# A diffusion layer in three-pass matmuls: the first up blocks reordered, the last output tile split over two free banks

## The chip, the cores and the metric

The kernel runs on one core of one Trainium2 chip. The metric is the device time of one execution in microseconds (us); for the kernel before it is the median of three runs. PE is TensorE's matmul row and PEld its weight loads, DVE is VectorE, ACT is ScalarE, POOL is GpSimd, and SP is SyncE, which here issues nearly all DMAs. SBUF is the on-chip working memory, PSUM the eight accumulation banks that PE writes.

## The reference, cut to what matters

One layer of a diffusion backbone over 1024 latent tokens of width 1024 with 256 context tokens, in float32. Two token mixers (retention and differential attention) are followed by an output projection, a norm, a gated feed-forward block with a convolution over the tokens, and a final norm. The change touches only what comes from the second norm on:

```python
def conv_ffn(h, w_up, conv_w, conv_b, w_down):
    u = h @ w_up                                   # (1024, 1024) @ (1024, 5632)
    up = jnp.pad(u, ((0, 0), (1, 1), (0, 0)))
    u = up[:, :-2] * conv_w[0] + up[:, 1:-1] * conv_w[1] + up[:, 2:] * conv_w[2] + conv_b
    a, b = jnp.split(u, 2, axis=-1)
    return (jax.nn.silu(a) * b) @ w_down           # (1024, 2816) @ (2816, 1024)

    h2 = rms_norm(x, norm2_g[l]) * (1.0 + sc2) + sh2
    x = x + g2 * conv_ffn(h2, w_up[l], conv_w[l], conv_b[l], w_down[l])
    return rms_norm(x, final_g)
```

## The kernel before, in words

**Arithmetic.** A float32 operand is split into a high part (a cast to fp32r on ACT, L1008) and a low part (the difference, on DVE, L1009); `passes` (L129 to L131) multiplies high by high, high by low and low by high into one PSUM bank. So a product of 128 x 512 over an inner size of 512 is 12 matmuls. Both projections of the feed-forward block use a seven-product (Strassen-like) scheme on halves, so the operands of products are sums and differences of quadrants of activations and weights.

**Up blocks.** There are 22 blocks of 128 output columns (`Block`, j = 0 to 21). For block j two weight tiles are loaded, `wra` (the columns of the gate half) and `wrb` (those of the other half), each 128 x 8 x 128. For j = 0 and 1 POOL forms the sums of weights ahead (`sums_in_place`); from j = NSUM = 2 on `combined` (L1163 to L1166) forms four of them on POOL, s1 = b1 + b2 first. The right weights of block 2 have a place of their own, `third_b`, which lies in memory that the first activation quadrants occupied. `begin` computes p1 and p2; `first_sum` copies the bank `chain` to `ua` (L1149) and adds p2 on DVE (L1150). `middle` adds p6 to the same bank, copies it to the right half of `ua` (L1250), adds p7 and copies it to the right half of `ub` (L1258). `end` adds p3 and p4 and finishes `ua` (L1265) and the left half of `ub` (L1266). A bank that is copied can be added to only when the copy is done. `ua` has two buffers, so block j + 2 takes that of block j. `gated` runs the convolution of both halves (ACT L1201, DVE L1202 and L1203), Silu on ACT (L1271), the product (L1272) and the stores of sums for the down projection (`down_operands`). In the loop the order is begin(j), end(j - 1), gated(j - 1), middle(j). The first three blocks' p1 and p2 and the third and fifth products of blocks 0 and 1 are computed earlier, while the turned activations T1 to T4 are still being split (`turned1`).

**Down projection.** Four phases over M = 11 pairs of blocks follow, each on the eight banks `c1` and `c2` (four row tiles each). Phase one multiplies a11 and a12 with the left weights, phases two and three the stored sums with differences of weights (`first_difference`, `less`), phase four the pair a22. All four quadrants of w_down for a pair, `W[m, r, c]`, are loaded in phase one's loop (L1351) and stay. At phase ends banks are copied or added into `acc`, one tile per 128 rows. `residual` loads the old row half from x1_d (L1380), multiplies by the gate and adds (L1382, L1383), and squares on ACT (L1385); `rstd` adds the two halves' sums (L1388) and takes the power on POOL (L115); `scaled` multiplies by the root and by the final gain and stores (L1393, L1394). In phase four the last four pairs are done tile by tile, so that four tiles of the lower half end one after another; tile 7 is the last.

**Order.** Instructions of one engine run in order. The order on each engine comes from a planner, which weighs costs and due times, except where `in_order` ties each instruction to the one before it on its engine (PE, DVE, ACT, SP). SP's queue is in order too: a DMA that waits for a buffer holds those behind it.

Of the kernel before, what the change touches and what calls it, by code (L numbers as in the profile page):

```python
# [8 lines left out]
F32 = mybir.dt.float32  # L9
# [3 lines left out]
ALU = mybir.AluOpType  # L13
# [59 lines left out]
def kernel(  # L73
# [39 lines left out]
    def rsqrt(out_ap, in_ap, mul, eps, n):  # L113
        nc.vector.tensor_scalar(out=out_ap, in0=in_ap, scalar1=mul, scalar2=eps, op0=ALU.mult, op1=ALU.add)  # L114
        nc.gpsimd.tensor_tensor(out=out_ap, in0=out_ap, in1=mhalf[:, :n], op=ALU.pow)  # L115

    def in_order(start):
        last = {}
        for ins in nc.cur_bb.bb.instructions[start:]:
            if ins.engine not in FORCE:  # L120
                continue
            if ins.engine in last:
                tc.add_manual_dep(ins, last[ins.engine].name, mybir.DependencyInfo(mybir.DependencyClass.NoSync, mybir.DependencyReason.DATA), reason="order")
            last[ins.engine] = ins
# [879 lines left out]

    def split_op(src):
        hi = wop.tile([P, 4, P], F32R, name="whi")
        lo = wop.tile([P, 4, P], F32R, name="wlo")
        nc.scalar.copy(hi, src)  # L1008
        nc.vector.tensor_tensor(out=lo, in0=src, in1=r32(hi), op=ALU.subtract)  # L1009
        return hi, lo  # L1010

    def raw_load(name, src, pool=None):
        o = (pool or wst).tile([P, KD, P], F32, name=name)
        nc.sync.dma_start(out=o, in_=src)
        return o
# [15 lines left out]
    xo = x1lS.enter_context(tc.tile_pool(name="xo", bufs=1, side="right"))  # L1031
    x1 = [(x1lp if t < 4 else x1hp).tile([P, D], F32, name=f"x1_{t}") for t in range(NT)]
    raw0 = rwp.tile([P, KD, 512], F32, name="raw0")
# [4 lines left out]
    def norm2(t):  # L1038
        nc.sync.dma_start(out=x1_d[t], in_=x1[t])
        sq = xo.tile([P, D], BF16, name="sq2")  # L1040
        nc.scalar.activation(sq, x1[t], AF.Square, accum_out=sm2[:, t : t + 1])
# [153 lines left out]
    with ExitStack() as p4:  # L1195
# [9 lines left out]

        third_b = p4.enter_context(tc.tile_pool(name="third_b", bufs=1, side="right", reuse_waits="tile"))
        raws.append(up_load(NSUM))
        held = {}

# [18 lines left out]
        class Block:  # L1228
# [4 lines left out]
            def op(self, p):  # L1233
                return split_op(self.ops[p])

# [11 lines left out]
            def middle(self):  # L1247
                j = self.j
                product(self.chain, self.op("p6"), T2, False)
                nc.scalar.copy(self.ua[:, 512:], self.chain)  # L1250
# [7 lines left out]
                nc.scalar.copy(self.ub[:, 512:], self.chain)  # L1258
                nc.vector.tensor_tensor(out=self.ub[:, 512:], in0=self.fifth, in1=self.ub[:, 512:], op=ALU.add)
# [7 lines left out]

            def gated(self):
                ta = conv(self.ua, self.j)
                tb = conv(self.ub, self.j + NF)  # L1270
                nc.scalar.activation(ta, ta, AF.Silu)  # L1271
                nc.vector.tensor_tensor(out=ta, in0=ta, in1=tb, op=ALU.mult)  # L1272
                down_operands(self.j, ta)

        last = None
        for j in range(NF):
            if NSUM < j + 1 < NF:
                raws.append(up_load(j + 1))
            blk = Block(j)
            blk.begin()  # L1280
            if last is not None:
                last.end()
                last.gated()
            blk.middle()
            last = blk
        last.end()
# [17 lines left out]
        for m in range(2):  # L1304
# [5 lines left out]
            for i, cc in enumerate((c1, c2)):  # L1310
                step(cc, split1(pa[:, i * C : (i + 1) * C]), split1(pb[:, i * C : (i + 1) * C]), m == 0, False)
        last.gated()
    ctx_t.close()
    ctx_y.close()
    ctx_ya.close()

    with ExitStack() as p5:
# [28 lines left out]
        W = {}  # L1346
        for m in range(2, M + 2):
            m %= M
            for r, c in ((0, 0), (1, 0), (0, 1), (1, 1)):
                W[m, r, c] = resident(F32)  # L1350
                nc.sync.dma_start(out=W[m, r, c], in_=w_down[2 * m + r][:, c * C : (c + 1) * C])  # L1351
            if m >= 2:
                a11, a12 = a_pair(0, m, alone=m < 4)
                step(c1, a11, split1(W[m, 0, 0]), False, m == M - 1)
                step(c2, a12, split1(W[m, 1, 0]), False, m == M - 1)
            if m >= 6:
                first_difference(m - 4)
        first_difference(0)
        first_difference(1)

# [4 lines left out]
        nc.sync.dma_start(out=fg, in_=rows[0, R_FG : R_FG + D].partition_broadcast(P))  # L1365
        sm4 = fin.tile([P, NT, 2], F32, name="sm4")
        halves = [slice(0, C), slice(C, D)]
# [9 lines left out]

        def residual(t, c, src=None):
            xt = fin.tile([P, C], F32, name="x1t", bufs=4)
            nc.sync.dma_start(out=xt, in_=x1_d[t][:, halves[c]])  # L1380
            dst = acc[t][:, halves[c]]
            nc.vector.tensor_tensor(out=dst, in0=dst if src is None else src, in1=g2bc[:, halves[c]], op=ALU.mult)  # L1382
            nc.vector.tensor_tensor(out=dst, in0=dst, in1=xt, op=ALU.add)  # L1383
            jk = fin.tile([P, C], BF16, name="jk", bufs=2)
            nc.scalar.activation(jk, dst, AF.Square, accum_out=sm4[:, t, c : c + 1])  # L1385

        def rstd(t):
            nc.vector.tensor_tensor(out=sm4[:, t, 0:1], in0=sm4[:, t, 0:1], in1=sm4[:, t, 1:2], op=ALU.add)  # L1388
            rsqrt(sm4[:, t, 0:1], sm4[:, t, 0:1], 1.0 / D, EPS, 1)

        def scaled(t, c0, c1_):
            x_ = acc[t][:, c0:c1_]
            nc.vector.scalar_tensor_tensor(out=x_, in0=x_, scalar=sm4[:, t, 0:1], in1=fg[:, c0:c1_], op0=ALU.mult, op1=ALU.mult)  # L1393
            nc.sync.dma_start(out=out[t * P : (t + 1) * P, c0:c1_], in_=x_)  # L1394
# [5 lines left out]
        for m in range(M):  # L1400
# [14 lines left out]
        for m in range(M):  # L1415
# [7 lines left out]
            T4s.append((hi, lo))  # L1423
        add_to(c1, 1, 1)
        add_to(c2, 0, 1)

        def rows_before(m):
            if m < 4:
                residual(m, 1)
                rstd(m)  # L1430
                scaled(m, 0, D)
                residual(4 + m, 1)
                dst = acc[4 + m][:, C:]
                nc.vector.tensor_tensor(out=dst, in0=dst, in1=fg[:, C:], op=ALU.mult)

        a22s = []
# [5 lines left out]
        late_ops = list(zip(a22s, T4s))[M - 4 :]  # L1442
        for t in range(4):
            for i, ops in enumerate(late_ops):
                step(c1, *ops, False, i == 3, True, [t])
            r = 4 + t
            residual(r, 0, c1[t])
            rstd(r)
            nc.scalar.activation(acc[r][:, C:], acc[r][:, C:], AF.Copy, scale=sm4[:, r, 0:1])
            nc.sync.dma_start(out=out[r * P : (r + 1) * P, C:], in_=acc[r][:, C:])  # L1450
            scaled(r, 0, C)

# [81 lines left out]
```

## Time and profile before

| what | us |
|---|---|
| median of 3 runs (1408.39 to 1412.42) | 1408.58 |
| the profiled execution, its own time | 1407.91 |
| its span | 1406.1 |
| busy DVE, ACT, POOL in the span | 991.4, 729.6, 287.5 |
| mean granted clock of TensorE | 0.995 |

A profile is of one execution. A line of the timeline gives start, duration, engine, source line, operation, output <- inputs, shape, and in brackets how long the engine was idle before it and what released it. A group line gives a count, busy us and mean ns of one, then the idle time before. Lines of DMA issues give the size and the median us from issue to landing. PE's matmul of 512 columns shows a duration of about 0.39 us, but the matmuls overlap: a new one starts every 0.23 us, and that step is what counts.

### The profile page before, as it was taken

The page shows a single profiled execution, that of the slowest core. Times are in us where ns is not written, and L with a number is a line of the kernel's source. Part 1 is how long each engine was busy: PE and PEld are TensorE (multiplying, and loading weights), DVE is VectorE, ACT ScalarE, POOL GpSimd, SP SyncE. Part 2 cuts the span into 40 slices and gives each one's busy share as a digit, 9 for nine tenths or more (in the row PEclk, how much of TensorE's full clock was granted, in tenths as well). Part 3 has the DMA queues.
Part 4 walks back from the last instruction along what each step waited for, and adds up shares of the span by engine and source line. Part 5 has one row for each costly group of instructions (what it writes and reads, how often), then busy time and mean ns, then how long its engine had stood idle before and what let it go on. Part 6 is the DMA issues. An engine that isn't in the chain of part 4 may idle for free.

```text
span 1406.1 us, 19426 instructions
## 1 busy us (share of the span) xinstructions
PE 1366.5 (97%) x7028; PEld 1147.6 (82%) x7028; DVE 991.4 (71%) x1445; ACT 729.6 (52%) x1391; POOL 287.5 (20%) x321
## 2 busy tenths in 40 slices
PE   8899999999999899999999999999999999999996
PEld 5688888888887799998888778888888888888885
DVE  3655874424686798886458987777787777897457
ACT  3553313333575689997136645555445555455533
POOL 1310000001656033411201242233332220000001
PEclk9999999999999999999999999999999999999999
DMA  9546885465575597622321223323323226953224
GB/s 336 224 151 200 284 278 188 134 182 172 177 242 159 175 208 170 126 66 85 141 98 45 97 98 113 113 90 113 105 105 113 96 79 219 397 175 104 91 97 179
DMA packets 96807, 218.81 MB, mean 156 GB/s; under 512 B 9220, under 2 KB 31236, under 8 KB 96200
## 3 DMA queue, kind: packets, MB, share of 16 engines
q1 hardware_dynamic: 88552, 192.67, 40.0%
q0 software_dynamic: 8160, 24.91, 7.8%
q8 instruction: 55, 0.90, 0.3%
q14 instruction: 40, 0.33, 0.1%
HBM read 160.13 MB, written 57.41 MB: 155 GB/s over the span
## 4 chain that ended last, share of the span: by engine, by line
PE 81%; issue 5%; DMA 5%; DVE 4%; ACT 2%; POOL 2%; SPq 0%; POOLq 0%; ACTq 0%; DVEq 0%
PE pv L869 5%; PE chain L129 5%; PE pA L837 5%; PE chain L131 5%; PE chain L130 5%; PE c L131 4%; PE c L129 4%; PE c L130 4%; PE pn L129 4%; PE pn L131 4%; PE pn L130 3%; PE pl L129 3%; PE pl L131 3%; PE pl L130 3%; PE third L129 2%
## 5 line engine op out<-in xcount | busy, mean ns | idle before, releaser
L129 PE MATMUL chain<-T,whi 128*128 128x512 f32 x264 | 103.5, 393 | 4.9 <-ACT ua L1250 3.9
L129 PE MATMUL pl<-hT,whi 128*128 128x512 f32 x256 | 106.2, 415 | 0.0
L130 PE MATMUL chain<-T,whi 128*128 128x512 f32 x264 | 103.5, 392 | 0.0
L131 PE MATMUL chain<-T,wlo 128*128 128x512 f32 x264 | 103.3, 392 | 0.0
L131 PE MATMUL pl<-hT,wlo 128*128 128x512 f32 x256 | 100.2, 391 | 0.0
L130 PE MATMUL pl<-hT,whi 128*128 128x512 f32 x256 | 100.0, 391 | 0.0
L840 DVE TENSOR_REDUCE mt<-pA 128x1 f32<-128x1280 f32 x64 | 95.3, 1490 | 3.6 <-PE pA L837 2.8
L837 PE MATMUL pA<-ks,qhl 128*128 128x512 f32 (+1 forms) x384 | 89.5, 369 | 2.7 <-ACT p L844 2.7
L131 PE MATMUL c<-whi,ghl 128*128 128x512 f32 x232 | 90.4, 390 | 0.0
L130 PE MATMUL c<-wlo,ghl 128*128 128x512 f32 x232 | 90.3, 389 | 0.0
L129 PE MATMUL c<-whi,ghl 128*128 128x512 f32 x232 | 90.3, 389 | 0.0
L844 ACT ACTIVATE p<-pA,mt 128x1280 f32<-128x1280 f32 x64 | 85.5, 1336 | 6.7 <-DVE mt L840 6.7
L1008 ACT CAST whi<-cmb 128x512 fp32r<-128x512 f32 x62 | 38.6, 623 | 86.7 <-PE chain L130 65.3
L837 PEld LDWEIGHTS pA<-ks,qhl 128*128 128x128 f32 x384 | 67.6, 189 | 14.8 <-ACT p L844 3.4
L129 PE MATMUL pn<-whi,hT 128*128 128x512 f32 x192 | 79.1, 412 | 0.0
L1163 POOL TENSOR_TENSOR cmb<-wrb 128x512 f32<-128x512 f32 x20 | 27.2, 1360 | 248.7 <-DMA wrb<-w_up 165.6
L869 PE MATMUL pv<-va,aT 128*128 128x128 f32 x640 | 77.0, 275 | 0.1
L131 PE MATMUL pn<-whi,hT 128*128 128x512 f32 x192 | 75.6, 394 | 0.9 <-POOL hT L552 0.4
L130 PE MATMUL pn<-wlo,hT 128*128 128x512 f32 x192 | 75.6, 394 | 0.0
L869 PEld LDWEIGHTS pv<-va,aT 128*128 128x128 f32 x640 | 74.0, 192 | 0.7 <-DVE yT L898 0.3
L1009 DVE TENSOR_TENSOR wlo<-cmb,whi 128x512 fp32r<-128x512 f32 x62 | 57.0, 922 | 23.0 <-ACT whi L1008 23.0
L115 POOL TENSOR_TENSOR sm<-sm,mhalf 128x1 f32<-128x1 f32 x26 | 17.0, 657 | 274.0 <-DVE sm L114 273.9
(300 smaller groups left out, 3812.7 us busy)
## 6 DMA issues: line engine op xcount, KB each, us to landing
wm<-w_mod SPq DMA_DIRECT2D x32, 512.0 KB, 5.1
raw<-w_in SPq DMA_DIRECT2D x27, 512.0 KB, 4.6
wra<-w_up SPq DMA_DIRECT2D x24, 512.0 KB, 3.4
wrb<-w_up SPq DMA_DIRECT2D x23, 512.0 KB, 3.5
W<-w_down SPq DMA_DIRECT2D x44, 256.0 KB, 6.2
ad<-s SPq DMA_DIRECT2D x20, 512.0 KB, 3.6
wra<-ad SPq DMA_DIRECT2D x20, 512.0 KB, 3.3
kvs<-kvg SPq DMA_DIRECT2D x36, 256.0 KB, 3.2
```

The lines of the kernel that those rows point to most:

```text
L115: nc.gpsimd.tensor_tensor(out=out_ap, in0=out_ap, in1=mhalf[:, :n], op=ALU.pow)
L129: mm(ps, lh, rh, start=first, stop=False, skip_group_check=more)
L130: mm(ps, lh, rl, start=False, stop=False, skip_group_check=more)
L131: mm(ps, ll, rh, start=False, stop=last, skip_group_check=more)
L837: mm(self.pa[m][:, c0:c1], self.q[:, m, i, qs], self.k[:, m, c0:c1], start=(i == 0), stop=(i == 1))
L840: nc.vector.tensor_reduce(out=self.mt[:, m : m + 1], in_=self.pa[m][:, :LK], axis=AX.X, op=ALU.min)
L844: nc.scalar.activation(self.p[m], self.pa[m][:, :LK], AF.Exp, scale=-1.0, bias=self.mt[:, m : m + 1], accum_out=self.s[:, m : m + 1])
L869: mm(self.pv, self.aT[:, c, :], self.v[:, c, :], start=(c == 0), stop=(c == NKT - 1))
L1008: nc.scalar.copy(hi, src)
L1009: nc.vector.tensor_tensor(out=lo, in0=src, in1=r32(hi), op=ALU.subtract)
L1163: nc.gpsimd.tensor_tensor(out=s1, in0=b1, in1=b2, op=ALU.add)
```

## The change

- `up_load(NSUM)`: block 2's right weights go into x1[7], the last row tile of the normed activations, which gets a pool of its own (`x1k`) and is kept to the end of the up blocks; `third_b` goes. The load is issued right after the first third products instead of after the pools of the first stage are closed. Its order against the left weights is no longer tied.
- The casts of block 2 are ordered behind block 0's copy of p7's bank (`copied[0]`).
- For j = 1, 2, 3 the call `last.gated()` moves behind `blk.middle()`, and its Silu is ordered behind the copy after p6 of block j (`blk.copied`).
- A one-column Silu is run on ACT in the first `norm2`, so that the table is loaded there.
- w_down: phase one loads only the left quadrants, the right ones (c = 1) for three pairs at its end and then for pair m + 3 in phase two, with `first_difference(m + 1)` there.
- `residual` is taken apart: `old_row` (load), `gated_row` (multiply and add), `squares`. Right halves of all eight tiles get gate and old row in phase three, left halves of tiles 0 to 3 too; what phase three adds is multiplied by the gate straight from the bank (`gated_more`) and added later (`add_more`). `rstd` takes the sum and the division in one instruction, with eps added ahead (`with_eps`).
- The end: tiles 4 to 6 as before, the four old rows loaded ahead; tile 7's part so far is taken from `c1[3]`, and its last four products go as two quarters of 256 columns into `c2[0]` and `c2[1]`. Its right half is stored from ACT's queue. The whole end is tied by `in_order`.

```diff
+    keptp = ctx.enter_context(ExitStack())
+    x1k = keptp.enter_context(tc.tile_pool(name="x1k", bufs=1, side="right", reuse_waits="tile"))
...
+    x1.append(x1k.tile([P, D], F32, name="x1_7"))
...
+        if t == 0:
+            nc.scalar.activation(sm2[:, 32:33], sm2[:, 0:1], AF.Silu)
...
         if j == NSUM:
-            start = len(nc.cur_bb.bb.instructions)
-            b = raw_load("wrb", w_up[j + NF], third_b)
-            a = raw_load("wra", w_up[j])
-            in_order(start)
-            return a, b
+            b = raw_load("wrb", w_up[j + NF], x1[NT - 1].rearrange("p (k l) -> p k l", k=KD))
+            return raw_load("wra", w_up[j]), b
...
     beside(iter(()), 0.0)
+    raws.append(up_load(NSUM))
     tmpS.close()
     rawp.close()
...
             def op(self, p):
-                return split_op(self.ops[p])
+                return split_op(self.ops[p], copied[0] if self.j == NSUM else None)
...
-            def gated(self):
+            def gated(self, after=None):
                 ta = conv(self.ua, self.j)
                 tb = conv(self.ub, self.j + NF)
-                nc.scalar.activation(ta, ta, AF.Silu)
+                silu = nc.scalar.activation(ta, ta, AF.Silu)
+                if after is not None:
+                    order_only(silu.ins, after.ins)
...
+            late_gate = 0 < j < 4
...
             if last is not None:
                 last.end()
-                last.gated()
+                if not late_gate:
+                    last.gated()
             blk.middle()
+            if late_gate:
+                last.gated(blk.copied)
...
+        for m in range(2, M):
+            load_W(m, 0)
+            a11, a12 = a_pair(0, m, alone=m < 4)
+            step(c1, a11, split1(W[m, 0, 0]), False, m == M - 1)
+            step(c2, a12, split1(W[m, 1, 0]), False, m == M - 1)
+        for m in range(2):
+            load_W(m, 0)
+        for m in range(3):
+            load_W(m, 1)
         first_difference(0)
...
-            if m < 4:
-                first_difference(M - 4 + m)
-            if 2 <= m < 6:
-                residual(m - 2, 0)
+            if m + 3 < M:
+                load_W(m + 3, 1)
+            if m + 1 < M:
+                first_difference(m + 1)
...
-        add_to(c1, 1, 1)
-        add_to(c2, 0, 1)
+            if m < NT:
+                t = (m + 4) % NT
+                gated_row(t, halves[1], acc[t][:, C:], old_row(t, 1))
+            if 2 <= m < 6:
+                gated_row(m - 2, halves[0], acc[m - 2][:, :C], old_row(m - 2, 0))
+                squares(m - 2, halves[0], 0)
+        late_rows = gated_more(c1, 1)
+        for row in late_rows:
+            add_more(*row)
+        first_rows = gated_more(c2, 0)
...
+        for n in range(2):
+            part = slice(n * C // 2, (n + 1) * C // 2)
+            for i, (a, b) in enumerate(late_ops):
+                passes(c2[n][:, : C // 2], tuple(g[:, 3 * P :] for g in a), tuple(g[:, part] for g in b), i == 0, i == 3)
+            gated_row(NT - 1, part, c2[n][:, : C // 2], acc[NT - 1][:, part], more[:, part])
+            squares(NT - 1, part, 2 * n)
+            if n == 0:
+                finish(NT - 2)
+                add_squares(NT - 1)
+        rstd(NT - 1, 2)
+        finish(NT - 1)
+        in_order(begin)
```

The helpers that are new: `order_only(a, b)` puts a behind b in the order without a semaphore; `finish(r)` scales and stores both halves of tile r; `gated_row`, `squares`, `gated_more`, `add_more` and `with_eps` are told above.

More of the change, by code (lines that the diff above doesn't have):

```diff
@@ L115, in rsqrt, with order_only @@
         nc.gpsimd.tensor_tensor(out=out_ap, in0=out_ap, in1=mhalf[:, :n], op=ALU.pow)
+    def order_only(ins, before):
+        tc.add_manual_dep(ins, before.name, mybir.DependencyInfo(mybir.DependencyClass.NoSync, mybir.DependencyReason.DATA), reason="order")
     def in_order(start):
@@ L122, in in_order @@
             if ins.engine in last:
-                tc.add_manual_dep(ins, last[ins.engine].name, mybir.DependencyInfo(mybir.DependencyClass.NoSync, mybir.DependencyReason.DATA), reason="order")
+                order_only(ins, last[ins.engine])
             last[ins.engine] = ins
@@ L1031 @@
     xo = x1lS.enter_context(tc.tile_pool(name="xo", bufs=1, side="right"))
-    x1 = [(x1lp if t < 4 else x1hp).tile([P, D], F32, name=f"x1_{t}") for t in range(NT)]
+    x1 = [(x1lp if t < 4 else x1hp).tile([P, D], F32, name=f"x1_{t}") for t in range(NT - 1)]
+    x1.append(x1k.tile([P, D], F32, name="x1_7"))
     raw0 = rwp.tile([P, KD, 512], F32, name="raw0")
@@ L1204, in conv @@
             return t
-        third_b = p4.enter_context(tc.tile_pool(name="third_b", bufs=1, side="right", reuse_waits="tile"))
-        raws.append(up_load(NSUM))
-        held = {}
+        held, copied = {}, []
         def down_operands(j, g):
@@ L1249, in middle @@
                 product(self.chain, self.op("p6"), T2, False)
-                nc.scalar.copy(self.ua[:, 512:], self.chain)
+                self.copied = nc.scalar.copy(self.ua[:, 512:], self.chain)
                 if j < NSUM:
@@ L1312 @@
         last.gated()
+    keptp.close()
     ctx_t.close()
@@ L1384, in residual, with squares @@
+        def squares(t, cols, i):
+            n = cols.stop - cols.start
             jk = fin.tile([P, C], BF16, name="jk", bufs=2)
[L1385 to L1389, printed above, removed]
+            nc.scalar.activation(jk[:, :n], acc[t][:, cols], AF.Square, accum_out=sm4[:, t, i : i + 1])
@@ new lines, in gated_row, with gated_more @@
+        def gated_row(t, cols, src, xt, tmp=None):
+            dst = acc[t][:, cols]
+            tmp = dst if tmp is None else tmp
+            nc.vector.tensor_tensor(out=tmp, in0=src, in1=g2bc[:, cols], op=ALU.mult)
+            nc.vector.tensor_tensor(out=dst, in0=tmp, in1=xt, op=ALU.add)
+        def gated_more(pd, r):
+            tmps = [fin.tile([P, C], F32, name="more", bufs=4) for _ in range(4)]
+            for t in range(4):
+                nc.vector.tensor_tensor(out=tmps[t], in0=pd[t], in1=g2bc[:, C:], op=ALU.mult)
+            return [(4 * r + t, tmps[t]) for t in range(4)]
@@ L1442, with finish @@
         late_ops = list(zip(a22s, T4s))[M - 4 :]
[L1443 removed]
+        olds = [old_row(4 + t, 0) for t in range(4)]
+        more = fin.tile([P, C], F32, name="more", bufs=4)
+        def finish(r):
+            nc.scalar.activation(acc[r][:, C:], acc[r][:, C:], AF.Copy, scale=sm4[:, r, 3:4])
+            (nc.scalar if r == NT - 1 else nc.sync).dma_start(out=out[r * P : (r + 1) * P, C:], in_=acc[r][:, C:])
+            scaled(r, 0, C)
+        begin = len(nc.cur_bb.bb.instructions)
+        for t in range(3):
+            r = 4 + t
             for i, ops in enumerate(late_ops):
                 step(c1, *ops, False, i == 3, True, [t])
[L1446 to L1451 removed]
+            gated_row(r, halves[0], c1[t], olds[t])
+            squares(r, halves[0], 0)
+            if t:
+                finish(r - 1)
+            else:
+                with_eps(NT - 1)
+                gated_row(NT - 1, halves[0], c1[3], olds[3])
+            rstd(r)
+        for n in range(2):
[10 more added lines that the diff above has]
+        in_order(begin)
 def shape_constants():
```

54 lines of the change are left out of this document (31 added, 23 removed).

## The prediction

> **What bounds the kernel now.** I read the page first: engine shares, then the forty slices.
>
> ```profile
> PE 1366.5 (97%) x7028; PEld 1147.6 (82%) x7028; DVE 991.4 (71%) x1445; ACT 729.6 (52%) x1391; POOL 287.5 (20%) x321
> ```
>
> PE is busy 97% of the 1406.1 us span, so a change that removes no matmul can only win what PE loses in waits. The change touches nothing before about 700 us; I therefore cut the rest of the span into stretches of 10 us. These are the only stretches behind 760 us in which PE loses more than 0.2 us (columns: stretch and its length, then busy us of PE, PEld, DVE, ACT, POOL, the granted clock, the DMA share, GB/s):
>
> ```profile
> 790.00:800.00 10.00, 7.13 (x31) 5.28 (x30) 7.41 (x7) 6.63 (x9) 8.81 (x6) 1.00 0.59 222
> 830.00:840.00 10.00, 8.08 (x28) 6.48 (x29) 7.18 (x10) 4.50 (x8) 3.01 (x2) 0.83 0.24 82
> 1390.00:1400.00 10.00, 4.86 (x22) 3.69 (x20) 8.34 (x18) 4.70 (x11) 2.10 (x3) 0.98 0.48 180
> 1400.00:1406.10 6.10, 0.00 (x0) 0.00 (x0) 1.06 (x3) 0.89 (x3) 0.55 (x1) 0.50 0.46 172
> ```
>
> Two losses sit at the start of the up blocks (one of them with a lowered clock), one at the end. The view of waits, for PE from 740 us on, has two lines in all:
>
> ```profile
> PE chain L129 <- ACT ua L1250: 3.9, 2, 2.1
> PE chain L129 <- ACT ub L1258: 1.0, 1, 1.0
> ```
>
> All three waits are for ScalarE's copy of a bank which PE wants to go on adding to. Between 840 and 1390 us, where phases one to four of the down projection lie, there is nothing to win, only to lose.
>
> **First stalls (790 to 800 us).** Timeline of ACT, and of PE at the second stall:
>
> ```profile
> 792.88 0.62 ACT L1008 CAST whi<-cmb 128x512 fp32r<-128x512 f32 x1 [1.06 <-POOL cmb L1164]
> 793.40 0.58 ACT L1258 COPY ub<-chain 128x512 f32<-128x512 f32 x1
> 796.22 1.28 ACT L1271 ACT_TABLE_LOAD   x1 [1.72 <-DVE tconv L1203]
> 798.95 0.59 ACT L1250 COPY ua<-chain 128x512 f32<-128x512 f32 x1
> 797.34 0.39 PE L131 MATMUL chain<-T,wlo 128*128 128x512 f32 x1
> 799.59 0.50 PE L129 MATMUL chain<-T,whi 128*128 128x512 f32 x1 [1.86 <-ACT ua L1250]
> ```
>
> ACT works in order. Block 0's copy (793.40) stands behind a cast for block 2 that waits for a sum on POOL; block 1's copy (798.95) stands behind a table load and a Silu that wait for DVE's convolution. The change puts the casts of block 2 behind the first copy, the Silu behind the second, and pulls the table load forward to the first norm. The built order agrees: ACT now has copy, cast, cast, block 2's first copy, cast, copy, copy, then convolution and Silu.
>
> The 1.0 us wait goes. The 2.0 us wait (799.59 less 797.34 less one matmul of 0.23) does not go wholly, because ACT now stands one step earlier: block 2's first copy writes the buffer of block 0, which is free only when DVE has read it.
>
> ```profile
> 794.62 1.52 DVE L1203 SCALAR_TENSOR_TENSOR tconv<-ua,cl,tconv 128x1023 f32<-128x1023 f32 x1
> ```
>
> That is at 796.14. The copy (0.58) ends near 796.7, and a cast, a copy and block 1's copy follow at about 0.5 each, the last done near 798.3. PE has its next matmuls (four of block 1, four of block 2, then block 1's next product) waiting from 796.2: gaps of about 0.5 and 0.6, and perhaps 0.1 behind the Silu, 1.2 in place of 3.0. That is 1.8 us won.
>
> **What the early load of block 2 costs.** Its right weights now go into x1[7], free after the last transposes, instead of memory that is free at 786 us.
>
> ```profile
> 773.16 0.60 PE L1048 MATMUL pt<-ident,x 128*128 128x128 f32 x4
> 786.20 0.33 SPq L1014 DMA_DIRECT2D wrb<-w_up  x1
> 790.17 1.30 POOL L1163 TENSOR_TENSOR cmb<-wrb 128x512 f32<-128x512 f32 x1 [31.12 <-DMA wrb<-w_up]
> 757.77 1.29 POOL L1160 TENSOR_TENSOR cmb<-wrb,wra 128x512 f32<-128x512 f32 x1
> 757.87 1.74 DVE L1009 TENSOR_TENSOR wlo<-wrb,whi 128x512 fp32r<-128x512 f32 x1 [0.70 <-ACT whi L1008]
> 784.85 0.68 DVE L1009 TENSOR_TENSOR wlo<-wra,whi 128x512 fp32r<-128x512 f32 x1
> 785.75 0.40 PE L131 MATMUL chain<-T,wlo 128*128 128x512 f32 x1
> ```
>
> Issue can come at 773.8, and with today's 3.97 us from issue to POOL's start the sum falls near 777.8, into a stretch in which DVE starts an operation every 0.60 us without a hole. Beside a POOL sum (757.77) the DVE operation at 757.87 took 1.74 against 0.68, so DVE loses 1.06. Its result of 784.85 is ready at 785.53 and PE uses it at 785.75: 0.22 slack, so PE waits 0.84 there, a new wait. Bounds: 0, if the sum falls beside something that doesn't collide, and 1.3, the whole sum. I take 0.84. On SP the load of block 2's left weights is queued behind this wait, but it needs its own buffer, read last at 784.85, so it moves from 786.6 only to 785.6 or, with the delay, not at all. The first region is worth 1.8 - 0.84 = 1.0 us, between -0.5 (collision 1.3, gaps 2.2) and 2.5 (no collision, 0.5 of gaps).
>
> **Third stall (829 to 836 us).**
>
> ```profile
> 826.97 0.39 PE L129 MATMUL third<-yT,whi 128*128 128x512 f32 x1
> 829.46 0.39 PE L131 MATMUL third<-yT,wlo 128*128 128x512 f32 x1
> 831.92 0.50 PE L129 MATMUL chain<-T,whi 128*128 128x512 f32 x1 [2.07 <-ACT ua L1250]
> 836.34 0.43 PE L129 MATMUL chain<-yT,whi 128*128 128x512 f32 x1
> 827.47 1.25 ACT L1201 ACTIVATE tconv<-ub,cl 128x1024 f32<-128x1024 f32 x1
> 830.34 1.06 ACT L1271 ACTIVATE tconv<-tconv 128x1024 f32<-128x1024 f32 x1 [1.62 <-DVE tconv L1203]
> 831.30 0.57 ACT L1250 COPY ua<-chain 128x512 f32<-128x512 f32 x1
> ```
>
> A product is 12 matmuls; 826.97 to 829.46 holds 11 steps, 0.2264 each. The gap costs 2.46 - 0.23 = 2.2 us. Then 12 matmuls take from 831.92 to 836.34, 4.42 in place of 2.72: 1.7 us for the lowered clock. Now the Silu goes behind the copy. The copy then follows the convolution of 827.47 and one cast: it ends near 829.7, where PE wants it at 829.69. PE will be some 1.0 us earlier, DVE and ACT somewhat less; I charge 0.3, too small a gap for the clock, and count 3.6. Bounds 0 and 3.9. Behind the late Silu stand DVE's product and the stores of the block, which are read only in phase one, 350 us later.
>
> The clock row next to a rule: the Trainium skill ("TensorE: Matmul & The Clock Gate", "What's actually happening") says the clock falls after an idle window of about 3.4 us. Here it fell behind a gap of 2.46, which does not agree. By that rule the gap would not be the cause and the 1.7 us would stay (estimate 6.3 us won in all, not 8.0).
>
> **The tail.** The chain of waits from PE's last matmul, in time:
>
> ```profile
> 1394.47 0.39 PE L131 MATMUL c<-W,wlo 128*128 128x512 f32 x1
> 1396.98 0.68 DVE L1382 TENSOR_TENSOR acc<-c,g2bc 128x512 f32<-128x512 f32 x1
> 1399.46 0.61 ACT L1385 ACTIVATE jk<-acc 128x512 bf16<-128x512 f32 x1
> 1400.62 0.55 POOL L115 TENSOR_TENSOR sm<-sm,mhalf 128x1 f32<-128x1 f32 x1 [1.82 <-DVE sm L114]
> 1401.21 0.75 DVE L1393 SCALAR_TENSOR_TENSOR acc<-acc,sm,fg 128x512 f32<-128x512 f32 x1 [0.67 <-POOL sm L115]
> 1402.38 0.38 SPq L1394 DMA_DIRECT2D out_dram<-acc  x1
> ```
>
> From 1394.86 it takes 2.1 us until DVE is free for the last tile, 1.8 more until ACT is through the other tile, and the two last stores go one behind the other on SP. Now the last tile's four late products go as two quarters of 256 columns into two free banks. Prices at this width, from an earlier stage:
>
> ```profile
> 112.75 0.28 PE L131 MATMUL pc<-cT,wlo 128*128 128x256 f32 x1
> 115.98 0.28 PE L131 MATMUL pc<-cT,wlo 128*128 128x256 f32 x1
> L286 DVE TENSOR_TENSOR yr<-pyt,yr 128x256 fp32r<-128x256 f32 x16 | 6.7, 420 | 6.9 <-ACT yr L285 6.9
> L407 ACT CAST xhl<-pc 128x256 fp32r<-128x256 f32 x4 | 1.5, 372 | 6.2 <-DMA dk<-xhl 6.0 <-PE pc L131 0.3
> ```
>
> Step 3.23/28 = 0.115: 24 matmuls take 2.77, not 2.72, and PE ends at 1394.9 as before. The old rows are loaded ahead and the other rows' sums are done in phases three and four, so DVE has only tile 6's scaling (0.75) and the first quarter before it; I put the second quarter's product at 1395.95 (bounds 1395.0, free at once, and 1396.98, as late as now). Then two operations of 0.42, overlapped, to 1396.7; a square of about 0.4 and its small steps to POOL in 0.85 (now 1.16 for the double width and one step more): 1397.55; power 0.6, scaling 0.75: 1398.9. One store each on SP and ACT; from issue to the end of the span now 1406.1 - 1402.38 = 3.7, so 1402.6. Won: 3.4, between 2.4 and 4.4.
>
> **Edits costed at nothing.** The table load (1.28) and tiny Silu on ACT in the first norm wait for POOL; behind them stands only the next square, before which ACT is idle:
>
> ```profile
> 719.45 1.06 ACT L1041 ACTIVATE sq<-x 128x1024 bf16<-128x1024 f32 x1 [4.30 <-DVE x L1096]
> W<-w_down SPq DMA_DIRECT2D x44, 256.0 KB, 6.2
> ```
>
> Uncovered they would cost about 2 us. Right weights of w_down: of 44 loads of 6.2 us, 16 move into phase two, three iterations ahead of their use; an iteration is 24 x 0.2264 = 5.4 us, so the lead is 16 us. SP's queue carries them between the loads of the activations; the built order even has them earlier. Uncovered, see the third rival. The 12 row updates moved into phase three are two DVE operations of 0.68 each, 16 us over 60 us of matmuls.
>
> Sum: 1.0 + 3.6 + 3.4 = 8.0 us off the profiled execution's 1407.91 (span 1406.1): 1399.9. The median of the runs, 1408.58, is 0.67 above it: 1400.6.
>
> **Rivals.**
> 1. The third stall stays, as DVE's backlog holds the second convolution of block 2 and with it the copy. For it: DVE is full from 800 to 830 us and wins little of what PE wins. Against: the Silu was the last thing in front of the copy. Won 1.0 + 3.4: 1404.2. Chance 0.14.
> 2. The clock falls anyway, since the gap was not its cause or one of the smaller gaps trips it: 8.0 - 1.7, 1402.3. For it: the fall began 1 us behind the gap. Against: it is the only one behind 760 us until PE stops, and the 2.0 us gap had none. Chance 0.08. (It is what the rule of the Trainium skill above would give.)
> 3. Slower: right weights land late in phase two. Decides below a lead of 6.2 plus four steps (0.68, 0.68, 0.62, 0.68), 8.9 us, so if SP holds a load for over 7 us. Landing one iteration ahead costs 0.8 to 3.4 us in each of 8 iterations; halfway, 17 us: 1417.6. Against it: SP holds nothing but buffer waits met two iterations ahead. Chance 0.05.
> 4. Cleaner: the early sum collides with nothing and DVE is free at once at the end: 1.8 + 3.9 + 4.4 = 10.1: 1398.5. Chance 0.15.
>
> **How the numbers follow.** My forecast has the remaining 0.58, with a range of its own of 1398.7 to 1402.6. A difference counts from 0.3%, 4.2 us, so faster is below 1404.35: forecast nearly whole (0.56), rivals 2 and 4, half of rival 1: 0.86. Same: 0.09. Slower: 0.05. The range runs from 1397.4 (rival 4 with the first region at 2.5 and the run scatter) to 1404.3 (rival 1).
>
> **What would show it.** After: PE in 790 to 800 above 8.5; no stall over 1 us and clock 1.00 from 800 to 840; a PE wait near 786 with POOL's first sum of block 2 near 778; no wait of PE between 860 and 1390; about 7.7 us from PE's last matmul to the end, not 11.2. Wrong would be a gap before the copy of block 3, a clock below 1 before the tail, or PE short in phase two.

## The result, and the profile after

The changed kernel takes 1403.99 us (median of 12 runs, 1402.37 to 1408.14) against 1408.47 of the kernel before (12 runs): a ratio of 0.9964 with a 95% interval of 0.9954 to 0.9974, faster by 0.36%. The profiled execution took 1403.12 us, with a span of 1401.4. Of the 12 runs of after six, at a granted clock of 0.996 to 0.998, took 1402.37 to 1403.73 us, and six, at 0.994 or 0.995, 1404.25 to 1408.14.

The kernel before ran again beside each group of experiments, with medians of 1410.09 us (e1 to e4), 1409.15 (e5 to e8) and 1409.65 (e9 to e12). So times of different groups are compared by their ratios to it. e6, e7, e8, e10, e11 and e12 ran once each, with the profile; what is said of them is read from one execution.

The page of after gives the engines' shares, then the view of waits all that PE waited for from 740 us on (engine, line, what it waited for: us in total, times, longest):

```profile
PE 1366.3 (97%) x7040; PEld 1148.0 (82%) x7040; DVE 999.9 (71%) x1458; ACT 729.3 (52%) x1394; POOL 298.3 (21%) x321
```

```profile
PE c L132 <- ACT ghl L1346: 1.4, 1, 1.4
PE c L134 <- DVE ghl L1347: 0.5, 1, 0.5
PE chain L132 <- ACT ua L1156: 0.5, 1, 0.5
PE chain L132 <- ACT ua L1256: 0.3, 1, 0.3
```

POOL's busy time rose by 10.8 us with the same 321 instructions; one of them, the first sum of the weights loaded early, is 11.9 us longer by itself (below). The waits for the copies of the up blocks shrank from 4.9 us to 0.8, but two waits for `ghl`, the split activations of phase one, are new. The stretches of 10 us, with columns as before:

```profile
790.00:800.00 10.00, 9.24 (x39) 6.81 (x38) 8.59 (x10) 5.35 (x10) 7.95 (x6) 1.00 0.52 184
830.00:840.00 10.00, 10.00 (x44) 7.96 (x43) 9.90 (x11) 3.98 (x7) 3.89 (x3) 1.00 0.24 79
1200.00:1210.00 10.00, 8.10 (x35) 6.09 (x34) 5.37 (x7) 4.70 (x7) 0.00 (x0) 1.00 0.77 267
1390.00:1400.00 10.00, 2.88 (x25) 2.68 (x23) 5.56 (x13) 4.09 (x10) 1.65 (x3) 0.87 0.56 210
```

PE is full at 830 us at clock 1.00, where it had 8.08 at 0.83. At 1200 us, where nothing was lost before, 1.9 us are missing.

To see where the time went, each trace is cut at three rows of PE: the start of the last output-projection matmul, the start of the down projection's first, and the start of its last. For after all three, with the row ahead of the place of the third stall (828.83) between them, then the first two of before, whose third is 1394.47 (timeline of PE):

```profile
755.16 0.39 PE L134 MATMUL po<-wohi,yT 128*128 128x512 f32 x1
...
828.83 0.39 PE L134 MATMUL third<-yT,wlo 128*128 128x512 f32 x1
...
1174.85 0.39 PE L132 MATMUL c<-whi 128*128 128x512 f32 x1
...
1392.61 0.28 PE L134 MATMUL c<-W,wlo 128*128 128x256 f32 x1
```

```profile
753.90 0.39 PE L131 MATMUL po<-wohi,yT 128*128 128x512 f32 x1
...
1179.14 0.39 PE L129 MATMUL c<-whi 128*128 128x512 f32 x1
```

The same cut for all kernels run (us; "up" and "down" are the distances between the rows, "end" is from the last row to the end of the span):

| kernel | first row at | up | down | end | span |
|---|---|---|---|---|---|
| before | 753.90 | 425.24 | 215.33 | 11.63 | 1406.1 |
| after | 755.16 | 419.69 | 217.76 | 8.79 | 1401.4 |
| e1 fin below dop | 756.25 | 419.68 | 219.70 | 8.77 | 1404.4 |
| e2 no early load | 755.61 | 420.47 | 215.30 | 8.72 | 1400.1 |
| e3 up blocks alone | 753.77 | 419.67 | 219.38 | 11.68 | 1404.5 |
| e4 down projection alone | 754.54 | 425.14 | 215.28 | 8.74 | 1403.7 |
| e5 e1 with sm4 of 512 bytes | 755.78 | 419.66 | 215.30 | 8.76 | 1399.5 |
| e6 block 2's gate back | 756.16 | 421.58 | 217.78 | 8.78 | 1404.3 |
| e7 a hole on DVE | 755.89 | 420.34 | 219.12 | 8.75 | 1404.1 |
| e8 casts back | 756.76 | 420.90 | 217.79 | 8.75 | 1404.2 |
| e9 ua free first | 753.93 | 420.40 | 215.28 | 8.79 | 1398.4 |
| e10 block 0's gate back | 755.93 | 422.33 | 218.10 | 8.74 | 1405.1 |
| e11 table load back | 753.91 | 419.65 | 219.27 | 8.77 | 1401.6 |
| e12 last stores on SP | 754.76 | 419.68 | 219.17 | 8.79 | 1402.4 |

Most of what differs in "first row at", 753.8 to 756.8, is scatter between executions, as it differs between kernels that are the same up to there. It arises early: from PE's 2501st matmul (486.20 us in before, 487.45 in after) to that row it is 267.7 us in all fourteen. So the table load in the first norm, which lies in this stretch, cost PE nothing there. Without the scatter the change won 5.55 us in the up blocks and 2.84 at the end, and lost 2.43 in the down projection: 5.96, of which 1.26 of scatter leave the 4.7 by which the spans differ.

### The profile page after: what moved, and what is told of

Read it like the earlier page. It is cut to its first block, busy times and chain, and to the rows that moved or that the text cites. A ratio compares the mean times of both kernels' runs of the same rounds, so it can differ in the third digit from the quotient of the medians.

```text
span 1401.4 us, 19449 instructions
## 1 busy us (share of the span) xinstructions
PE 1366.3 (97%) x7040; PEld 1148.0 (82%) x7040; DVE 999.9 (71%) x1458; ACT 729.3 (52%) x1394; POOL 298.3 (21%) x321
## 4 chain that ended last, share of the span: by engine, by line
PE 82%; DVE 7%; DMA 4%; issue 3%; POOL 2%; ACT 2%; SPq 0%; POOLq 0%; ACTq 0%; DVEq 0%
PE chain L132 5%; PE chain L133 5%; PE chain L134 5%; PE pv L872 5%; PE pA L840 5%; PE c L134 4%; PE c L132 4%; PE c L133 4%; PE pn L132 4%; PE pn L134 4%; PE pn L133 4%; PE pl L134 3%; PE third L132 3%; PE third L133 3%; PE pl L132 3%; PE third L134 3%
## 5 line engine op out<-in xcount | busy, mean ns | idle before, releaser
L1014 DVE TENSOR_TENSOR wlo<-cmb,whi 128x512 fp32r<-128x512 f32 x62 | 60.5, 976 | 20.3 <-ACT whi L1011 20.3
L1011 ACT CAST whi<-wra 128x512 fp32r<-128x512 f32 x55 | 33.7, 622 | 72.9 <-PE third L133 42.6
```

Source lines behind the costliest of these rows:

```text
L1011: cast = nc.scalar.copy(hi, src)
```

## Experiments

**The new stall in phase one.** Timeline of after for ACT and PE; the stores of s34 there by their line; and ACT in the kernel before:

```profile
1202.86 1.04 ACT L1346 CAST ghl<-wra 128x1024 fp32r<-128x1024 f32 x1 [4.76 <-DMA ad<-s]
...
1203.96 0.50 PE L132 MATMUL c<-whi,ghl 128*128 128x512 f32 x1 [1.38 <-ACT ghl L1346]
...
1205.21 0.50 PE L134 MATMUL c<-whi,ghl 128*128 128x512 f32 x1 [0.53 <-DVE ghl L1347]
```

```profile
L1232 POOL DMA_DIRECT2D ad<-s x1: 533/533/533, 1194.9 to 1194.9; - x1
...
who waited for it (us, times):
  ACT ghl L1346: 4.8, 1
...
DMA to landing us min/median/max: 3.4/4.2/7.9
```

```profile
1203.21 1.06 ACT L1333 CAST ghl<-wra 128x1024 fp32r<-128x1024 f32 x1 [0.79 <-DMA ad<-tconv]
1207.48 1.05 ACT L1333 CAST ghl<-wrb 128x1024 fp32r<-128x1024 f32 x1 [3.21 <-DMA ad<-s]
```

A cast into `ghl` waits for a store of `s`, a tile that it has nothing to do with but the memory: the pool of `ghl` (dop) is laid where the pool of the up blocks was, and the last store of `s`, issued from POOL, lands 7.9 us after its issue at 1194.9. Before, it was the second `ghl` tile that waited for this store, and PE needed it late enough. After, by the code, x1[7] lies under the pool of the up blocks and is given back with it, so against the tiles of that pool phase one's pools begin 4 KB a partition further down than before, and now it is the first tile that waits.

e1 swaps the two pools, so that `ghl` comes to lie elsewhere:

```diff
-        dop = p5.enter_context(tc.tile_pool(name="dop", bufs=2, side="right", reuse_waits="tile"))
         fin = p5.enter_context(tc.tile_pool(name="fin", bufs=1, side="right", reuse_waits="tile"))
+        dop = p5.enter_context(tc.tile_pool(name="dop", bufs=2, side="right", reuse_waits="tile"))
```

> Theory (place): in the changed kernel the first ghl tile of phase one lies where the last sums s are still being stored, and waits for a store that lands 7.9 us after its issue. Here only the two pools of phase one change places (fin below, dop above), so no ghl tile lies there. Expected: the first ghl cast starts some 4 us earlier than in the changed kernel (before 1200 us), no PE wait between 1190 and 1215 us, time about 2 us below the changed kernel's 1404.0, so 1402. Rival (queue): the stall comes from the weight loads of w_down that were moved, so the stall of 1.4 and 0.5 us stays and the time is 1404.

The waits of PE in e1, the first cast, and two stretches:

```profile
PE chain L132 <- ACT ua L1156: 0.5, 1, 0.5
PE chain L132 <- ACT ua L1256: 0.3, 1, 0.3
```

```profile
1190.69 1.05 ACT L1346 CAST ghl<-wra 128x1024 fp32r<-128x1024 f32 x1
```

```profile
1190.00:1200.00 10.00, 10.00 (x45) 8.03 (x44) 9.63 (x15) 6.11 (x10) 2.15 (x4) 1.00 1.01 355
...
1210.00:1220.00 10.00, 10.00 (x44) 8.10 (x43) 7.98 (x11) 3.65 (x6) 0.00 (x0) 1.00 0.97 349
```

The cast is 12 us earlier, and the stall is gone: the theory holds. But the time is 1405.28 us (10 runs, ratio 0.9969, 0.9957 to 0.9980), no better than the changed kernel's 0.9964, where 2 us less were expected. From the first `ghl` product on PE is busy without a gap at clock 1.00, but from 1210 to 1220 us the view counts 44 matmuls, where that of after has 46: the next run shows why.

e5 is e1 with the small tile `sm4` of fin, the pool that `ghl` now lies behind, four times as wide:

```diff
-        sm4 = fin.tile([P, NT, 4], F32, name="sm4")
+        sm4 = fin.tile([P, NT, 16], F32, name="sm4")
```

> As the run with fin below dop, but the small tile sm4 takes 512 bytes of a partition instead of 128, so that the ghl tiles begin 384 bytes further on. In the run with fin below dop the stall was gone, but from the first ghl product on a matmul started every 0.2324 us instead of 0.2267, 4.4 us over the down projection. Theory (address): the step is slower because ghl began at an odd multiple of 128 bytes; here it is 0.2267 again, the down projection takes 215.3 us from its first matmul to PE's last, and the ratio to the kernel before is about 0.994 (5.6 won in the up blocks, 2.9 in the tail). Rival: the step depends on which memory ghl lies in, or was a clock of that one execution; in the first case it stays at 0.2324 and the ratio at 0.997, in the second the two runs differ by nothing but scatter.

Groups by line in 1210 to 1380 us (count, busy us, mean ns of one), in e1 and then in e5:

```profile
L133 PE MATMUL c<-wlo,ghl 128*128 128x512 f32 x223 | 88.0, 395 | 0.0
```

```profile
L133 PE MATMUL c<-wlo,ghl 128*128 128x512 f32 x222 | 86.4, 389 | 0.0
```

In e1 the mean step from one start to the next was 0.2324 us from 1210 to 1375 us, in e5 0.2267, as everywhere else. Moving `ghl` by 384 bytes gave back 4.4 us of the down projection (219.70 to 215.30); e9, which has the same `sm4`, shows 215.28. So the place of `ghl` counts; that it is the odd multiple of 128 bytes, as the theory has it, is not shown, since only one shift was tried. e5 takes 1401.0 us (4 runs, ratio 0.9933, 0.9917 to 0.9950). No version has a lower ratio, though that of e9 can't be told from it, and the interval lies below that of the changed kernel (0.9954 to 0.9974).

e3 and e4 each take one half of the change: the functions up to phase one as after and the rest as before, and the reverse.

> The kernel before with the edits of the up blocks alone (early load, casts, late Silu, early table load); phases one to four as before, so all of w_down loads in phase one. Theory (place): the first stalls shrink from 3.0 to about 1.2 us, the third stall and the slow clock go (together 5.8 us won), and the phase-one stall of about 2 us is there, since the shift by 4 KB is: 1408.5 - 3.8 = 1404.7. Rival (queue): without the moved loads there is no phase-one stall: 1402.7.

> The kernel before with the edits of phases one to four alone (weight loads moved, rows and tail); up blocks as before. Theory (place): no stall in phase one, the tail wins 2.8 us and the moved loads nothing: 1405.7; stalls at 793, 797 and 830 us and the clock of 0.83 as before. Rival (queue): the moved loads bring the phase-one stall of 2 us: 1407.7.

PE's waits in e3, and in e4:

```profile
PE c L132 <- ACT ghl L1346: 1.6, 1, 1.6
PE c L134 <- DVE ghl L1347: 0.5, 1, 0.5
PE chain L132 <- ACT ua L1156: 0.5, 1, 0.5
PE chain L132 <- ACT ua L1256: 0.3, 1, 0.3
```

```profile
PE chain L129 <- ACT ua L1250: 3.9, 2, 2.1
PE chain L129 <- ACT ub L1258: 0.9, 1, 0.9
```

e3, with all weights of w_down still loaded in phase one, has the stall; e4, with the loads moved, has none, and its down projection takes 215.28 us, as before. So the moved loads neither cause the stall nor cost anything. e3 takes 1406.32 us (0.9980, 0.9966 to 0.9994), by the medians 3.8 less than the kernel before in its group, which is the gain that was expected. Its profiled execution lost 4.05 us in the down projection, not 2.4, as the clock fell behind the stall (0.83 from 1200 to 1210 us). e4 takes 1406.46 us (0.9971, 0.9958 to 0.9985), 3.6 less, where 2.8 was expected; that lies within the interval.

**The early load.** e2 gives block 2's right weights their old load, order and place, and changes nothing else (the lines of the load):

```diff
-            b = raw_load("wrb", w_up[j + NF], x1[NT - 1].rearrange("p (k l) -> p k l", k=KD))
...
+            b = raw_load("wrb", w_up[j + NF], third_b.tile([P, KD, P], F32, name="wrb"))
```

> Block 2's right weights load at their old time into their old place; everything else as changed. Theory (port): the early load bought nothing, because POOL's first sum stood behind DVE's two-input operations until DVE was through at 791.6 us. Expected: POOL's sums of block 2 start near 790 to 791.5 us, PE's gaps between 790 and 802 us sum to 1.1 to 1.5 us as in the changed kernel, and without the shift by 4 KB the phase-one stall is gone too: 1402. Rival: the early load is what shortened the gaps; then they grow by 0.5 to 1.5 us, and the time is 1402.5 to 1403.5.

POOL and DVE in after, then POOL and a wait of PE in e2:

```profile
778.35 13.21 POOL L1170 TENSOR_TENSOR cmb<-x 128x512 f32<-128x512 f32 x1 [18.02 <-DVE yT L1066]
...
779.48 0.68 DVE L1066 TENSOR_TENSOR T<-raw,T 128x512 fp32r<-128x512 f32 x1
780.08 0.68 DVE L1128 TENSOR_TENSOR raw<-raw 128x512 f32<-128x512 f32 x1
...
789.71 0.68 DVE L1014 TENSOR_TENSOR wlo<-wrb,whi 128x512 fp32r<-128x512 f32 x1
790.32 0.68 DVE L1259 TENSOR_TENSOR ua<-fifth,ua 128x512 f32<-128x512 f32 x1
...
791.64 1.30 POOL L1171 TENSOR_TENSOR cmb<-cmb,wra 128x512 f32<-128x512 f32 x1
```

```profile
791.68 1.29 POOL L1170 TENSOR_TENSOR cmb<-wrb 128x512 f32<-128x512 f32 x1 [30.93 <-DMA wrb<-w_up]
...
804.78 0.50 PE L132 MATMUL chain<-T,whi 128*128 128x512 f32 x1 [0.99 <-ACT ub L1265]
```

The sum took 13.21 us instead of 1.29. It ends at 791.56, 1.24 us after DVE began its first operation that reads a PSUM bank (790.32, `fifth`). POOL alone takes 1.29 for it. So POOL got nothing as long as DVE ran operations with two SBUF inputs one behind the other, and DVE kept its step of 0.60. Still, counted from the first product with T (786.56 in after, 787.01 in e2), the sum was ready 1.0 us earlier than in e2, and that was worth 0.8 us: the up blocks take 420.47 us in e2, 419.69 in after, with a wait of 1.0 at 804 us that after doesn't have. The theory fell in this point (the rival's 0.5 to 1.5 is what was measured), while the phase-one stall went as expected: 1402.24 us (4 runs, 0.9943, 0.9921 to 0.9964).

e7 puts one small DVE operation that reads a PSUM bank into that stretch:

```diff
+            if c == 2:
+                hole = nc.vector.tensor_tensor(out=sm2, in0=chain[0][:, :64], in1=ident[:, :64], op=ALU.add)
...
```

> The changed kernel with one small DVE operation more (128 x 64, one input from a PSUM bank), placed into the stretch of two-input operations behind which POOL's first sum of block 2 stood for 13.2 us. Theory (port held): POOL gets in at that operation, so its sum ends about 1.3 us behind it, near 784 instead of 791.6 us, and a DVE operation beside it is 0.6 to 1.1 us longer. Rival (the port is shared out, POOL merely slow): the sum still ends near 791 us and no DVE operation is longer.

```profile
779.17 6.50 POOL L1175 TENSOR_TENSOR cmb<-x 128x512 f32<-128x512 f32 x1 [18.12 <-DVE yT L1066]
...
784.43 0.22 DVE L1147 TENSOR_TENSOR sm<-chain,ident 128x64 f32<-128x64 f32 x1
784.57 2.86 DVE L1066 TENSOR_TENSOR T<-raw,T 128x512 fp32r<-128x512 f32 x3
...
788.68 0.50 PE L134 MATMUL chain<-T,wlo 128*128 128x512 f32 x1 [0.78 <-DVE wlo L1014]
```

POOL gets in at the hole: its sum ends at 785.67, 1.24 us behind 784.43. Three DVE operations then take 2.86 us, 0.97 more than such a group did in after while POOL was shut out (1.89 from 781.89), and PE waits 0.78 us for a low part. That is the collision that the prediction had charged (0.84); it costs what was said, but in the kernel as changed it doesn't happen.

**The single edits of the up blocks.** Each run takes back one of them. Their edits are `late_gate = 0 < j < 3` (e6), `split_op(self.ops[p])` without the order (e8), `late_gate = 1 < j < 4` (e10) and `norm2` without its Silu (e11).

> The changed kernel, but the gate of block 2 stays in its old place (late for two blocks instead of three). Theory (gap sets the clock): the wait for the copy of block 3 is back near 830 us, 2.2 us long, and the clock of 0.83 with it, 1.7 us: 3.9 us in all over the changed kernel. Rival (the fall of the clock was no matter of that gap): a gap of 2.2 us with full clock, 2.2 us in all. Second rival: PE's earlier waits being gone, DVE's backlog is smaller or the order another, and the wait is under 1 us.

> The changed kernel without the order of block 2's casts behind block 0's copy. Theory: the cast that waits for POOL's second sum (done near 793 us) stands in front of the copy again, so PE's wait of 1.0 us for ub near 793 us is back, and no other. Rival: since the first sum is there at 791.6 us, as before, but the convolution moves behind the casts too, the loss is larger, 1.5 to 2.5 us.

> The changed kernel, but the gate of block 1 aside: that of block 0, which comes in the loop of block 1, stays in its old place (late for j = 2 and 3 only). Theory: ACT's Silu, which waits for DVE's convolution, stands in front of block 2's and block 1's copies again, but the table load is gone, so of the 2.0 us wait of the kernel before some 0.7 us (2.0 less 1.28) come back over the 1.1 us that the changed kernel loses there. Rival: the Silu was not what held the copies, as they wait for the buffer of ua: the loss stays at 1.1 us.

> The changed kernel without the early Silu, so the table (1.28 us) is loaded in the first gate, near 800 us. Theory: there it stands behind the copies that PE waits for, so it costs PE 0 to 0.5 us (at the copy for ub near 803 us), and up to the last output-projection matmul nothing changes. Rival: it costs its whole 1.28 us.

PE's rows in e6, e8 and e10, then ACT in e11:

```profile
832.16 0.50 PE L132 MATMUL chain<-T,whi 128*128 128x512 f32 x1 [1.93 <-ACT ua L1256]
```

```profile
797.37 0.50 PE L132 MATMUL chain<-T,whi 128*128 128x512 f32 x1 [1.48 <-ACT ub L1264]
```

```profile
800.43 0.69 PE L132 MATMUL chain<-T,whi 128*128 128x512 f32 x1 [1.87 <-ACT ua L1156]
```

```profile
798.28 1.26 ACT L1207 ACTIVATE tconv<-ub,cl 128x1024 f32<-128x1024 f32 x1
799.56 1.28 ACT L1275 ACT_TABLE_LOAD   x1
```

In the up blocks e6 costs 1.9 us, e8 1.2, e10 2.6 and e11 nothing. The first three bring a wait back at its place, so each of these orders is needed. In e6 it is 1.9 us long, but the clock stayed at 1.00 (first rival): the 1.7 us that the slow clock cost before don't hang on that wait alone. In e8 the wait is 1.5 us, between theory and rival: the convolution has indeed moved behind the cast. In e10 PE stands still for 2.0 us in place of 1.1 in two gaps, 0.9 more where 0.7 was expected; the other 1.7 are the clock, at 0.83 from 800 to 810 us, which was not. In e11 the table load (1.28) runs behind the copies that PE wants, so moving it ahead won nothing here.

e9 goes on from e5 and pulls block 0's convolution of `ua` on DVE in front of what stood between its two steps, to free the buffer that block 2's first copy waits for (`order_only` of the addition to `ub` and of block 2's low parts behind it).

> The run with fin below dop and sm4 of 512 bytes, and on DVE block 0's convolution of ua in front of block 0's addition to ub and of the low parts for block 2. In that run PE still waits 0.4 and 0.3 us behind 797 us, since block 2's first copy on ACT waits for the buffer of ua, which DVE reads last at the end of that convolution. Theory: the buffer comes free 0.6 us earlier, both waits go or halve, 0.4 to 0.8 us won: ratio about 0.9930. Rival: the low parts for block 2 come later instead and PE waits for those: no change, 0.9933, or a loss of up to 0.5 us.

```profile
794.08 2.20 DVE L1213 SCALAR_TENSOR_TENSOR tconv<-ua,cl,tconv 128x1023 f32<-128x1023 f32 x1
```

The step starts right behind the first, but beside a POOL operation it takes 2.20 us, not 1.72 as in after, and PE waits three times for copies, 1.2 us in all, instead of twice and 0.7. The up blocks take 420.40 us, 0.7 longer than in e5, the whole 1400.68 us (6 runs, 0.9936, 0.9922 to 0.9950): no gain over e5.

**The end.** e12 puts the last tile's two stores on one queue.

```diff
-            (nc.scalar if r == NT - 1 else nc.sync).dma_start(out=out[r * P : (r + 1) * P, C:], in_=acc[r][:, C:])
+            nc.sync.dma_start(out=out[r * P : (r + 1) * P, C:], in_=acc[r][:, C:])
```

> The changed kernel with the last tile's two stores one behind the other on SP instead of one on ACT and one on SP. Theory: a second issue behind the first costs 0.4 us or nothing, since with two queues the end came 4.2 us behind the issues and before, with one, 3.7 us behind the last: from PE's last matmul to the end 8.8 us as in the changed kernel, at most 9.2. Rival: one queue is quicker to land, 8.4 us.

Timeline of after, then of e12:

```profile
1396.42 0.75 DVE L1435 SCALAR_TENSOR_TENSOR acc<-acc,sm,fg 128x512 f32<-128x512 f32 x1 [0.66 <-POOL sm L1431]
1397.17 0.39 ACTq L1500 DMA_DIRECT2D out_dram<-acc  x1
```

```profile
1398.17 0.33 SPq L1500 DMA_DIRECT2D out_dram<-acc  x1
1398.60 0.38 SPq L1436 DMA_DIRECT2D out_dram<-acc  x1
```

In both the span (1401.4 and 1402.4) ends 4.23 us behind the first issue, 8.79 us behind the start of PE's last matmul. The second queue wins nothing.

## Why the prediction was right or wrong, step by step

Faster was right, and 1403.99 lies within the range. But it lies above the range of the forecast itself (1398.7 to 1402.6), and the likeliest value was 3.4 us too low: of 8.0 us forecast the medians show 4.5. By the profiles the three places won 8.4 us (1.9, 3.7 and 2.8), and 2.4 were lost where nothing had been charged. One term failed in the gains, one was mis-sized, and one loss was left out. That the time stayed in the range is partly luck: its upper end came from rival 1, a third stall that stays, which didn't come; and the 0.84 us charged for a collision that didn't come paid a third of the loss that did.

- **First stalls, forecast 1.0, measured 1.9.** From the first row to the last matmul ahead of the third stall PE took 75.56 us before (829.46 less 753.90) and takes 73.67 after (828.83 less 755.16). The gaps were read rightly: 1.2 us were left by the sum, 0.62 and 0.46 by the trace (797.38 to 798.23 and 799.03 to 799.72, less a step each), and the 1.8 that they were to win is what came. The step that failed is the collision of the early sum. The prediction let POOL in and charged DVE 0.84; POOL was shut out, and DVE lost nothing. e7 shows that the price was right and the event wrong. The row it was taken from (757.77) was one in which POOL had begun first.
- **Third stall, forecast 3.6, measured 3.7.** This is what is won from that matmul to phase one (349.68 us less 346.02). The copy (828.37 to 828.94 in after) is in time, no wait is left and the clock stays at 1.00. Up to the thirteenth matmul behind it 3.85 us are won (6.88 less 3.03); some 0.2 is lost again near 837, so that the 0.3 held in reserve was about right. Rivals 1 and 2 did not come. e6 confirms the wait's share (1.9); that its removal keeps the clock up is what the trace of after shows, but e6 doesn't show that its return brings the clock down.
- **Nothing to lose between 840 and 1390 us, forecast 0, measured -2.4.** This is the step that made the total too good. "Costed at nothing" went through engines and queues, not through memory: the change moved a pool, and with it what later tiles share with earlier ones. e1 and e2 take the stall away in two ways, e3 and e4 place it in the half of the change that leaves phase one's code alone. Rival 3 looked for a loss in the down projection too, but for late weights; the moved loads cost nothing (e4).
- **The tail, forecast 3.4, measured 2.84.** The chain to the scaling was nearly right: 4.56 us from the start of PE's last matmul to the issue of the stores, 4.3 by the sum. The term that was off is the store: 3.7 us was measured from the second issue of the kernel before, whose first came at 1401.96, 4.1 us ahead of the end, and two stores in one queue end no later than two in two (e12). The right term is 4.2 behind the first issue.
- **Scatter.** The kernels profiled here start the changed stretch between 753.8 and 756.8 us, which is as large as the terms in question. Of the eight profiles here that have the phase-one stall the clock fell behind it in four (e3, e7, e11, e12), which costs another 1.3 to 1.6 us. That the six longer runs of after are such executions fits, but was not shown.

## What to carry to other kernels

When a buffer gets a new place or a longer life, look at what every later pool then shares memory with: a tile whose writer starts by waiting for a store of another stage is found in the trace as an engine released by a DMA of a name that it doesn't use. An operation on POOL that is moved ahead, into a stretch where DVE runs two-input operations without a hole, gets ahead no further than the end of that stretch (here its result was ready 1.0 us earlier, not 13); its price and its worth both depend on whether it gets in. Cut the traces at rows that all variants have before differences of a few microseconds are read, since the scatter ahead of the change can be as large.

## What the runs showed of the hardware

- **POOL against DVE.** POOL's addition of 128 x 512 stood 12 us behind twenty DVE operations with two SBUF inputs, and ended 1.24 us behind the start of the first one that read PSUM; alone it takes 1.29. The Trainium skill ("SBUF — State Buffer", "SBUF: two separate sides") says that the port pair which the two share is locked for a whole instruction and that the other blocks; the rows agree (13.21 us without a hole, 6.50 with one), and add that an unbroken run of DVE operations does not let a waiting POOL operation in between.
- **The matmul's step depends on where its stationary operand lies** (the 128 x 128 block that PE loads ahead, here of `ghl`). With `ghl` behind a tile of 128 bytes a partition a matmul of 512 columns took a step of 0.2324 us (e1), with it 384 bytes further on 0.2267 (e5 and e9), at a granted clock of 1.00 in all.
- **The clock can fall behind waits of about 2 us, and not each time.** In e10 it was 0.83 over 800 to 810 us behind a gap of 2.0 us; in e6 a gap of 2.1 us left it at 1.00. The Trainium skill ("TensorE: Matmul & The Clock Gate", "What's actually happening") speaks of an activity window of about 3.4 us that runs on its own and of one idle window. Eight slow steps, seven of them of 0.427 us, as in the kernel before from 832.95 to 836.34, are 3.4 us, which agrees; but PE was not idle for a whole window in any of these cases (2.24 us at most at one wait).
